# A two-layer hybrid decoder trunk: zero-padded keys, weights in shared half slots, longer hidden groups

## The chip, the cores and the metric

The kernel runs on one core of one Trainium2 chip. The metric is the device time of one execution in microseconds (us), as the median of several runs. A core has five engines that each take instructions in their own order: TensorE (PE, matrix products; its weight loads are shown as PEld), VectorE (DVE), ScalarE (ACT), GpSimdE (POOL) and SyncE (SP, which here issues nearly all DMA transfers). They wait for each other by semaphores.

## What is computed

Two layers (`DEPTH = 2`) on an input of 512 tokens by 1024 features; `c` is a conditioning vector.

```python
for l in range(DEPTH):
    mod = jax.nn.silu(c) @ w_mod[l] + b_mod[l]
    sh1, sc1, g1, sh2, sc2, g2, sh3, sc3, g3 = jnp.split(mod[:, None, :], N_MOD, axis=-1)
    h = _rmsnorm(x) * (1.0 + sc1) + sh1
    x = x + HALF_STEP * g1 * _swiglu(h, ffn1_w_gate[l], ffn1_w_up[l], ffn1_w_down[l])
    h = _rmsnorm(x) * (1.0 + sc2) + sh2
    x = x + g2 * _hybrid_mixer(h, w_in[l], w_out[l], q_norm_g[l], k_norm_g[l], hgrn_norm_g[l], lower_bounds[l])
    h = _rmsnorm(x) * (1.0 + sc3) + sh3
    x = x + HALF_STEP * g3 * _swiglu(h, ffn2_w_gate[l], ffn2_w_up[l], ffn2_w_down[l])
```

`_swiglu` is `(silu(h @ w_gate) * (h @ w_up)) @ w_down` with 2816 hidden features, which are 22 blocks of 128. The mixer projects `h` to 3584 columns and runs three groups of heads: four heads of stick-breaking attention (a, 64 wide), four of dilated attention with normalised and rotated queries and keys (b, 64 wide), four of a gated linear recurrence (c, 128 wide). Their outputs meet in `w_out`.

## The kernel before

**Layout.** Activations lie transposed: features on the 128 partitions, 512 tokens along the free axis. `X` holds the residual stream as eight tiles of 128x512. Every matrix product is made of three (`triple`, line 865): each operand is split into a rounded high part and the remainder, and PE adds high x high, high x low and low x high in one PSUM bank. So a weight that arrives by DMA (tile `w`) needs an ACT copy that makes its high part and a DVE subtraction that makes its low part (tiles `wt`) before PE can use it.

**The program in stages.** `opening` (line 424) reads `x`, transposes it, forms the first layer's shift and scale in four rounds (`row_sums` on PE, `row_products` on DVE, `shift_scale`), modulates (`modulate`), and multiplies the first two pairs of weights (gate and up for blocks 0 and 1). Then come, per layer, a feed-forward network (`ffn`, line 1102), the mixer and a second feed-forward network; the four networks are numbered 0 to 3 in the text.

**A network** works through its 22 hidden blocks in pairs, and the pairs in groups of `GROUP = 6` blocks: 6, 6, 6, 4. For a pair, gate and up products are formed either in the plain way (`dense`: 96 products of 128x512 for gate and up together) or, for the pairs in `FAST`, by `seven` (line 874), which replaces eight block products by seven (168 products of 128x256) at the price of sums of weights and of activations that DVE makes (`combine`, line 943, and the "f" branch of `feed`), and `empty`, which takes the seven results apart. After a group, `down` (line 1212) multiplies its hidden blocks with `w_down` for each of the eight output tiles, and `residual` adds the gated result into `X` on DVE. In the last group the main stream first waits for all hidden blocks, loads the table of ACT functions, and starts the next norm (`start_norm`); its last four output tiles are done in two halves of 256 tokens, so that the norm of the first half can begin early.

**The mixer** starts its first two projections in halves (`first`), then runs the other twelve as filler beside four lanes of head tasks. For a pair of heads, queries and keys lie as one pair of tiles: head 0 in partitions 0 to 63, head 1 in 64 to 127. `stick` and `dilated` take the half that belongs to their head, so that these score products contract over 64 partitions.

**Modulation.** The other shift, scale and gate vectors come from 64 items of 1 MB of `w_mod`. `plan` (line 687) mixes these "mod" items into the list of weights (tables `TAKE` for networks, `TAKE_MIX` for mixers); `background` (line 730) multiplies and adds them on DVE into `acc`, two instructions of 128x1024 per item. A mod item keeps its raw buffer until DVE has done so; while a norm is under way (`hold`), its steps are put back by a bias of 5.0.

**Memory and order.** 37 slots of 4 KB per partition (`SLOTS`) hold activations and split weights (at most `HELD = 11` of them for weights), and three raw buffers of 8 KB (`RAW`) take the loads. `Flow` plays the program through with estimated costs as it is built: of all streams it takes the step that could begin first, with ranks and biases (`BU`, `BF`, `BH`, `BN`) between them. The order of instructions on each engine, the loads on SP too, is what comes out of that. All instructions are recorded by one helper, so that their line in the profile is the same (L111; in the changed kernel L114), and they are told apart by their tiles: `m` and `a` are PSUM banks, `h` the modulated input, `hs` its sums, `u` working tiles, `x` the residual stream.

## Time and profile before

| | |
|---|---|
| runs | 2170.59, 2169.46, 2168.57 us: median 2169.46 us |
| profiled execution | 2170.17 us; first to last instruction (span) 2168.4 us |
| TensorE clock granted, mean | 0.978 |
| PE busy | 2097.1 us (97%), 12592 matmul records |
| DVE busy | 1557.2 us (72%) |
| ACT busy | 979.0 us (45%) |
| POOL busy | 208.4 us (10%) |
| read from HBM | 255.25 MB, 119 GB/s over the span |

Times in the views are microseconds from the span's first instruction. A row of the timeline gives start, length, engine, operation with output and inputs, the count of instructions merged into it, and in brackets how long the engine had been idle before and what released it. A PE row's length includes the run-out of its last product, so paces are best taken from one start to the next. SPq is SP's time in issuing DMAs, waits included.

### The profile page before, as it was taken

What the parts mean: (1) busy time and instruction counts of PE and PEld (TensorE: products, weight loads), DVE (VectorE), ACT (ScalarE), POOL (GpSimd) and SP (SyncE); (2) the same over time, 40 slices, a digit from 0 to 9 for tenths busy, and PEclk for the clock granted to TensorE, in tenths of its full rate; (3) what the DMA queues carried; (4) which work ended last, traced back from release to release, by engine and by line L of the source; (5) the groups of instructions that cost most, each with busy time, mean ns of one, the idle gap of its engine ahead of it and who ended that gap; (6) DMA issues with size and microseconds to landing.
All of it is one profiled execution on the core that took longest, in us unless ns stands there. A gap on an engine that the chain in (4) does not pass through costs nothing.

```text
span 2168.4 us, 30995 instructions
## 1 busy us (share of the span) xinstructions
PE 2097.1 (97%) x12592; PEld 1858.2 (86%) x12592; DVE 1557.2 (72%) x2458; ACT 979.0 (45%) x1642; POOL 208.4 (10%) x235
## 2 busy tenths in 40 slices
PE   7999999899999999999999999998999999999998
PEld 6889989878787888898988989897888779898987
DVE  5866867787688776676785767578878968474665
ACT  3534434545565443433462424355465645242432
POOL 4000000131141100000010000012323201000000
PEclk7999999999999999999999999999999999999999
DMA  9435343353221343434334344333433212332322
GB/s 295 141 128 164 117 155 98 117 207 105 78 93 64 98 135 118 156 104 149 119 115 134 120 136 142 103 126 123 150 117 131 64 59 74 102 103 92 98 88 69
DMA packets 207007, 259.34 MB, mean 120 GB/s; under 512 B 5345, under 2 KB 188533, under 8 KB 206865
## 3 DMA queue, kind: packets, MB, share of 16 engines
q1 hardware_dynamic: 206608, 257.29, 36.4%
q8 instruction: 99, 1.62, 0.3%
q14 instruction: 44, 0.35, 0.0%
q0 software_dynamic: 256, 0.08, 0.0%
HBM read 255.25 MB, written 2.10 MB: 119 GB/s over the span
## 4 chain that ended last, share of the span: by engine, by line
PE 89%; DVE 7%; ACT 2%; DMA 1%; issue 1%; SPq 0%; POOL 0%; DVEq 0%; ACTq 0%
PE m L111 54%; PE a L111 35%; DVE u L111 3%; DVE wt L111 1%; ACT u L111 1%; DVE acc L111 1%; DMA w<-in_w_in_dram 1%; DVE h L111 1%; DVE x L111 0%; DMA u<-in_x_dram 0%; ACT wt L111 0%; DMA w<-in_ffn_w_down_dram 0%; SPq L111 0%; ACT L1351 0%; ACT L111 0%
## 5 line engine op out<-in xcount | busy, mean ns | idle before, releaser
L111 PE MATMUL m<-h,wt 128*128 128x512 f32 (+1 forms) x2928 | 585.5, 352 | 25.9 <-ACT wt L111 9.1
L111 PE MATMUL m<-u,wt 128*128 128x512 f32 (+1 forms) x2640 | 577.5, 376 | 10.7 <-DVE u L111 4.7
L111 PEld LDWEIGHTS m<-u,wt 128*128 128x128 f32 x2640 | 466.9, 190 | 101.8 <-ACT u L111 7.2
L111 PEld LDWEIGHTS m<-h,wt 128*128 128x128 f32 x2928 | 471.8, 195 | 94.6 <-ACT wt L111 9.5
L111 DVE TENSOR_TENSOR wt<-w,wt 128x1024 fp32r<-128x1024 f32 x458 | 502.6, 1112 | 68.2 <-ACT wt L111 67.3
L111 ACT CAST wt<-w 128x1024 fp32r<-128x1024 f32 x460 | 423.9, 950 | 249.2 <-DVE w L111 154.1
L111 PE MATMUL a<-h,wt 128*128 128x256 f32 (+1 forms) x2160 | 366.5, 325 | 0.0
L111 PEld LDWEIGHTS a<-h,wt 128*128 128x128 f32 x2160 | 321.8, 191 | 32.2
L111 DVE TENSOR_TENSOR u<-u 128x256 f32<-128x256 f32 (+4 forms) x448 | 254.9, 589 | 41.0 <-ACT u L111 25.0
L111 POOL TENSOR_TENSOR u<-u 128x256 f32<-128x256 f32 x162 | 140.8, 891 | 1350.5 <-ACT u L111 1104.9
L111 DVE SCALAR_TENSOR_TENSOR x<-m,mod,x 128x512 f32<-128x512 f32 (+1 forms) x168 | 115.1, 686 | 195.0 <-PE m L111 194.7
L111 PE MATMUL a<-hs,wt 128*128 128x256 f32 x1728 | 223.3, 283 | 0.0
L111 PEld LDWEIGHTS a<-hs,wt 128*128 128x128 f32 x1728 | 214.4, 192 | 0.0
L111 PE MATMUL a<-u 128*128 128x64 f32 (+8 forms) x1056 | 162.4, 299 | 5.1 <-DVE u L111 4.4
L111 PEld LDWEIGHTS a<-u 128*128 128x128 f32 (+1 forms) x1056 | 142.9, 193 | 26.9 <-issue 9.3
L111 ACT ACTIVATE u<-u 128x512 f32<-128x512 f32 (+2 forms) x266 | 145.1, 567 | 36.8 <-POOL u L111 14.0
L111 DVE SCALAR_TENSOR_TENSOR acc<-w,sc_c,acc 128x1024 f32<-128x1024 f32 x112 | 145.6, 1300 | 4.6 <-DMA w<-in_w_mod_dram 2.3
L111 ACT COPY u<-m 128x256 f32<-128x256 f32 (+1 forms) x109 | 45.1, 415 | 227.2 <-PE m L111 218.9
L111 ACT CAST u<-u 128x512 fp32r<-128x512 f32 (+1 forms) x105 | 64.5, 617 | 157.6 <-DVE u L111 157.4
L111 DVE TENSOR_TENSOR w<-w 128x512 f32<-128x512 f32 x192 | 131.9, 687 | 3.0
L111 DVE TENSOR_TENSOR u<-u,a 128x256 f32<-128x256 f32 (+1 forms) x88 | 47.3, 539 | 97.7 <-PE a L111 89.6
L111 PE MATMUL m<-wt,h 128*128 128x256 f32 x768 | 100.8, 288 | 5.9 <-DVE u L111 4.8
(136 smaller groups left out, 1382.3 us busy)
## 6 DMA issues: line engine op xcount, KB each, us to landing
w<-in_w_mod_dram SPq DMA_DIRECT2D x64, 1024.0 KB, 5.0
w<-in_ffn_w_gate_dram SPq DMA_DIRECT2D x44, 1024.0 KB, 5.4
w<-in_ffn_w_up_dram SPq DMA_DIRECT2D x44, 1024.0 KB, 5.4
w<-in_ffn_w_down_dram SPq DMA_DIRECT2D x48, 768.0 KB, 4.4
w<-in_w_in_dram SPq DMA_DIRECT2D x28, 1024.0 KB, 5.1
u<-in_w_mod_dram SPq DMA_DIRECT2D x32, 256.0 KB, 6.2
w<-in_ffn_w_down_dram SPq DMA_DIRECT2D x16, 512.0 KB, 3.5
w<-in_w_out_dram SPq DMA_DIRECT2D x8, 512.0 KB, 3.9
```

Of the source, the lines that this page charges most:

```text
L111: ins = fn(*args, **kw)
```

## The change

Five things change, and with them the whole order that `Flow` makes:

1. **Keys per head.** Keys of groups a and b now get one tile per head, with zeros in the rows of the other head (`halves_of_keys`; POOL writes the zeros, ACT and DVE write the 64 rows). The score products contract over all 128 partitions, against the unsplit query tiles.
2. **Raw weights in half slots.** The three raw buffers are gone; a load takes one or two slots of 4 KB from the common pool, now of 43 slots, with at most 8 raw slots in networks and 4 in mixers (`RAW = (8, 4)`). A load of 1 MB becomes two DMAs of 512 KB, each slot is given back by itself, and the split of a "seven" weight follows these halves.
3. **Opening without GpSimd products.** `x * rsqrt` and the second weight's low parts, which POOL made, go to DVE; `modulate` is DVE, ACT, DVE; the splits stand one by one between the rounds.
4. **Modulation with networks only.** 24, 16, 20 and 4 mod items go with networks 0 to 3, spread by a formula, none with the mixers.
5. **Groups 8, 8, 6.** `FAST` has five pairs in network 0 and six in the others, from pair 4 on, and never the last pair. The first two output tiles of each group take the group's last two hidden blocks only after all others (`down_two`), and the table load before a norm is a stream of its own, which the main stream does not wait for. `Flow` also counts PE as slower after a pause.

```diff
-SLOTS = 37
+SLOTS = 43
 RESERVE = 4
-RAW = 3
+RAW = (8, 4)
 HELD = (11, 11)
...
-GROUP = 6
-FAST = ((6, 8, 12, 14, 18, 20),) * 4
+GROUPS = (8, 8, 6)
+FAST = ((4, 8, 12, 16, 18), (4, 8, 10, 12, 16, 18), (4, 8, 10, 12, 16, 18), (4, 8, 10, 12, 16, 18))
...
+MOD_NET = (24, 16, 20, 4)
+EARLY = ((2, 4, 5, 6), (1, 3, 4, 6), (1, 3, 4, 6), (1, 3, 4, 6))
+MOD_MIX = ((0,) * 14,) * 2
...
-            t += self.cost(eng, op, out, ins)
+            if eng == "PE" and t - self.clk[eng] > 1.3:
+                self.cold = t + 3.2
+            t += self.cost(eng, op, out, ins) * (1.9 if eng == "PE" and t < self.cold and out.free_size() > 128 else 1.0)
...
-        xr = [U.get() for _ in range(ND)]
-        for d in range(ND):
-            G.tensor_mul(xr[d], X[d], junk)
...
-            A.activation(t, xr[d], AF.Identity, scale=mod(0, 1, d), bias=mod(0, 0, d))
-            A.copy(hi, t)
-            V.tensor_sub(lo, t, hi)
-            U.put(xr[d])
+            V.scalar_tensor_tensor(t, X[d], mod(0, 1, d), junk, ALU.mult, ALU.mult)
+            A.activation(hi, t, AF.Identity, bias=mod(0, 0, d))
+            V.scalar_tensor_tensor(lo, t, mod(0, 0, d), hi, ALU.add, ALU.subtract)
...
+        split(0, 0)
         modulate(0)
-        split(raw[0], V)
         modulate(1)
-        split(raw[1], G)
...
     def load(i):
-        r = RW.get()
         it = items[i]
...
+        r = [RW.get() for _ in range(slots_of(it))]
+        if it[0] == "mod":
             _, l, j, q = it
...
+            for k in range(2):
+                Q.dma_start(r[k], w_mod[l, (2 * q + k) * P:(2 * q + k + 1) * P, j * D:(j + 1) * D])
+            return r
...
             def down(w, d, cs):
...
+            def down_two(w, cuts):
+
+                yield Step("PE", need=((M, 2),))
+                banks = [M.get() for _ in range(2)]
+                for ks in cuts:
+                    for d, ps in enumerate(banks):
+                        for k in ks:
+                            yield when(keys[k])
+                            hi, lo = hid[k]
+                            wh, wl = part(w, k, d)
+                            yield Step("PE", lo, wh, wl)
+                            triple(ps, wh, wl, hi, lo, k == 0, k == n - 1)
+                        if ks[-1] == n - 1:
+                            F.spawn(residual(key, d, ps, l, jg, FULL), 0)
...
-                for i in range(2):
-                    yield from down(w, d + i, FULL)
+                if d == 0:
+                    yield from down_two(w, (range(n - 2), range(n - 2, n)))
+                else:
+                    for i in range(2):
+                        yield from down(w, d + i, FULL)
...
+        def halves_of_keys(name, hp, src, first):
+
+            tiles = [U.whole(name="k") for _ in range(2)]
+            for j, t in enumerate(tiles):
+                G.memset(t[64 - 64 * j:128 - 64 * j].bitcast(F32), 0.0)
+            for j, t in enumerate(tiles):
+                o = slice(64 * j, 64 * j + 64)
+                first(t[o, :S], src[o])
+            for j, t in enumerate(tiles):
+                o = slice(64 * j, 64 * j + 64)
+                yield Step("DVE", src, t)
+                V.tensor_sub(t[o, S:], src[o], t[o, :S])
+            got[name, hp] = tiles
...
-            qh, ql = (z[r:r + 64] for z in got["qa", hp])
-            kh, kl = (z[r:r + 64] for z in got["ka", hp])
+            qh, ql = got["qa", hp]
+            kt = got["ka", hp][h % 2]
+            kh, kl = kt[:, :S], kt[:, S:]
```

Three places show what becomes of the order; the rows name operation, output and inputs, shape and count.

The first is SP's queue of loads where network 0 ends and the first mixer begins (`w` is a raw buffer, behind the arrow stands the tensor in HBM). Before:

```order
L111 DMA w<-in_w_mod_dram 128x2x1024
L111 DMA w<-in_ffn_w_down_dram 128x4x256 x4
L111 DMA w<-in_w_in_dram 128x8x256
L111 DMA w<-in_w_mod_dram 128x2x1024
L111 DMA w<-in_w_in_dram 128x8x256
L111 DMA w<-in_w_mod_dram 128x2x1024 x2
L111 DMA w<-in_w_in_dram 128x8x256
```

And in the changed kernel:

```order
L114 DMA w<-in_w_mod_dram 128x1024 x2
L114 DMA w<-in_ffn_w_down_dram 128x4x256
L114 DMA w<-in_ffn_w_down_dram 128x2x256
L114 DMA w<-in_ffn_w_down_dram 128x4x256
L114 DMA w<-in_ffn_w_down_dram 128x2x256
L114 DMA w<-in_ffn_w_down_dram 128x4x256
L114 DMA w<-in_ffn_w_down_dram 128x2x256
L114 DMA w<-in_w_in_dram 128x4x256 x28
```

The mod loads that stood between the projections' weights are gone: all 28 halves of the fourteen projections follow each other.

The second is DVE in the opening, from the first shift and scale (`mod`) to the third; `acc` is a row product, `h` the low part of the modulated input, `wt` the low part of a weight. Before:

```order
L111 TENSOR_TENSOR mod_94<-a,bcol_96 128x2x2
L111 TENSOR_TENSOR h<-u,h 128x512
L111 TENSOR_TENSOR wt<-w,wt 128x1024 x2
L111 TENSOR_TENSOR h<-u,h 128x512
L111 TENSOR_SCALAR acc<-u,sc_c 128x512
L111 SCALAR_TENSOR_TENSOR acc<-u,sc_c,acc 128x512 x4
L111 TENSOR_TENSOR mod_94<-a,bcol_96 128x2x2
L111 TENSOR_TENSOR h<-u,h 128x512 x2
L111 TENSOR_SCALAR acc<-u,sc_c 128x512
L111 SCALAR_TENSOR_TENSOR acc<-u,sc_c,acc 128x512 x5
L111 TENSOR_TENSOR mod_94<-a,bcol_96 128x2x2
```

And in the changed kernel, up to the second:

```order
L114 TENSOR_TENSOR mod_91<-a,bcol_93 128x2x2
L114 TENSOR_TENSOR wt<-w,wt 128x1024
L114 SCALAR_TENSOR_TENSOR u<-x_83,mod_91,u 128x512
L114 SCALAR_TENSOR_TENSOR h<-u,mod_91,h 128x512
L114 SCALAR_TENSOR_TENSOR u<-x_84,mod_91,u 128x512
L114 SCALAR_TENSOR_TENSOR h<-u,mod_91,h 128x512
L114 TENSOR_TENSOR wt<-w,wt 128x1024
L114 TENSOR_SCALAR acc<-u,sc_c 128x512
L114 SCALAR_TENSOR_TENSOR acc<-u,sc_c,acc 128x512 x4
L114 TENSOR_TENSOR mod_91<-a,bcol_93 128x2x2
```

Each modulated tile now takes two instructions of DVE, where it took one.

The third is PE at the end of network 0: the first two output tiles of the last group (banks `m_3324` and `m_3344` before, `m_3273` and `m_3274` after; behind the arrow a hidden block `u`, then the high and the low part of a half of `w_down`, `wt`). Before, each bank takes the group's four blocks in a row:

```order
L111 MATMUL m_3324<-u_3127,wt_3182 128x512 x2
L111 MATMUL m_3324<-u_3127,wt_3183 128x512
L111 MATMUL m_3324<-u_3150,wt_3182 128x512 x2
L111 MATMUL m_3324<-u_3150,wt_3183 128x512
L111 MATMUL m_3324<-u_3317,wt_3182 128x512 x2
L111 MATMUL m_3324<-u_3317,wt_3183 128x512
L111 MATMUL m_3324<-u_3303,wt_3182 128x512 x2
L111 MATMUL m_3324<-u_3303,wt_3183 128x512
L111 MATMUL m_3344<-u_3127,wt_3182 128x512 x2
```

And in the changed kernel, from the fourth of the group's six blocks in the second bank:

```order
L114 MATMUL m_3274<-u_3097,wt_3116 128x512 x2
L114 MATMUL m_3274<-u_3097,wt_3117 128x512
L114 MATMUL m_3273<-u_3231,wt_3181 128x512 x2
L114 MATMUL m_3273<-u_3231,wt_3182 128x512
L114 MATMUL m_3273<-u_3281,wt_3181 128x512 x2
L114 MATMUL m_3273<-u_3281,wt_3182 128x512
L114 MATMUL m_3274<-u_3231,wt_3181 128x512 x2
L114 MATMUL m_3274<-u_3231,wt_3182 128x512
L114 MATMUL m_3274<-u_3281,wt_3181 128x512 x2
L114 MATMUL m_3274<-u_3281,wt_3182 128x512
```

The last pair's two blocks (`u_3231`, `u_3281`) now stand behind 24 products of the other four; before, the last pair's two (`u_3317`, `u_3303`) stood behind six.

## The prediction, made before the change was run

> **What bounds the kernel now.** I read the page's totals and chain first, then stretches of the span by windows, then the PE rows of the timeline where those stretches fall short.

> ```profile
> PE 2097.1 (97%) x12592; PEld 1858.2 (86%) x12592; DVE 1557.2 (72%) x2458; ACT 979.0 (45%) x1642; POOL 208.4 (10%) x235
> PE 89%; DVE 7%; ACT 2%; DMA 1%; issue 1%; SPq 0%; POOL 0%; DVEq 0%; ACTq 0%
> ```

> PE carries 89% of the chain. But a busy PE need not be at its pace, so I took the pace from two links of the chain, and then one network against the two mixers (columns: length, then busy time of PE, PEld, DVE, ACT, POOL, then the granted clock):

> ```profile
> 92.80 10.88 PE m L111 x48
> 157.54 10.08 PE a L111 x84
> 120.00:378.00 258.00, 258.00 (x1615) 234.42 (x1614) 183.74 (x287) 105.10 (x168) 0.00 (x0) 1.00 0.41 132
> 440.00:730.00 290.00, 281.53 (x1629) 239.76 (x1628) 234.81 (x415) 156.54 (x280) 67.34 (x81) 0.95 0.34 113
> 1500.00:1790.00 290.00, 279.57 (x1647) 238.15 (x1648) 236.51 (x422) 157.78 (x287) 68.85 (x76) 0.97 0.33 109
> ```

> 48 products of 512 columns in 10.88 us are 0.2267 us each; 84 of 256 columns in 10.08 are 0.120. The difference gives 0.417 us per 1000 columns and 13 ns per product; "at pace" means this below. Network 0 is full, at clock 1.00: there only fewer columns help. The mixers lack 8.5 and 10.4 us of PE and run at clock 0.95 and 0.97: 290 x 0.05 + 290 x 0.03 is another 23 us. So what can be won lies in the mixers, at their starts, at the networks' ends and in the opening.

> **The change part by part.** The sum is made against the profiled execution, 2170.2 us, which is 0.7 above the median.

> *Keys per head.* PE gets as many products and columns, over 128 rows in place of 64.

> ```profile
> L111 PE MATMUL a<-u 64*128 64x512 f32 x48 | 12.8, 460 | 0.0
> 548.12 0.80 PE L111 MATMUL a<-u 64*128 64x384 f32 x3
> 551.70 1.75 PE L111 MATMUL a<-u 128*128 128x512 f32 x5
> 695.63 0.55 PE L111 MATMUL a<-u 64*128 64x128 f32 x3
> 696.11 0.96 PE L111 MATMUL m<-u,wt 128*128 128x512 f32 x3
> 671.74 2.17 PE L111 MATMUL a<-u 64*128 64x512 f32 x15
> 673.84 1.66 PE L111 MATMUL m<-u,wt 128*128 128x512 f32 x6
> ```

> A stick head's scores (from 548.12 to 551.70: four triples of 64 rows and four 128-column products between them) take 3.58 us. At pace they are 3 x 1280 columns x 0.417/1000 + 12 x 0.013 + 4 x 0.112 = 2.3, so 1.24 are lost; eight heads make 9.9. A lone dilated triple (695.63 to 696.11) takes 0.48 against 3 x 0.067 = 0.20; with the entry I call it 0.35 (an estimate), and some ten per mixer make 3.5. The burst of fifteen goes the other way: 2.10 us against 15 x 0.2267 = 3.40, so its loss of 1.3 per mixer is the change's. Together -9.9 - 7.0 + 2.6 = **-14** (bounds: all of the first two, -17; the sticks' without their strict products, -8).

> [...]

> *The clock behind those bursts.*

> ```profile
> 500.00:530.00 30.00, 29.94 (x190) 25.58 (x188) 25.30 (x40) 17.11 (x32) 1.57 (x1) 0.92 0.46 147
> 530.00:560.00 30.00, 30.00 (x133) 24.32 (x132) 16.58 (x32) 20.31 (x38) 5.32 (x8) 0.86 0.07 29
> 560.00:600.00 40.00, 37.51 (x186) 31.57 (x186) 29.15 (x44) 20.45 (x34) 10.31 (x13) 0.91 0.32 106
> 1590.00:1620.00 30.00, 30.00 (x136) 24.63 (x136) 21.82 (x36) 22.07 (x38) 7.28 (x9) 0.89 0.37 127
> ```

> Where the stick heads run, the granted clock falls to 0.86 to 0.92, in 530 to 560 with PE busy throughout. Time lost: 30 x 0.08 + 30 x 0.14 + 40 x 0.09 + 30 x 0.11 = 13.5. If 64-row products count as little work to what grants the clock, full-height ones end this; the window of 560 also has 2.5 us of idle PE. I take half, **-7** (0 to -13.5).

> [...]

> *Mixer starts.* This is where SP's queue changes.

> ```profile
> 389.12 14.52 SPq L111 DMA_DIRECT2D w<-in_w_mod_dram  x2
> 420.04 0.37 SPq L111 DMA_DIRECT2D w<-in_w_in_dram  x1
> 424.88 5.92 PE L111 MATMUL a<-h,wt 128*128 128x256 f32 x48
> 435.35 1.22 PE L111 MATMUL m<-h,wt 128*128 128x512 f32 x2 [4.54 <-ACT wt L111]
> 438.89 12.64 PE L111 MATMUL m<-h,wt 128*128 128x512 f32 x46 [2.33 <-DVE wt L111]
> 451.38 0.30 PE L111 MATMUL a<-p,quads 128*128 128x32 f32 x2
> 1487.13 5.92 PE L111 MATMUL a<-h,wt 128*128 128x256 f32 x48
> 1501.08 10.98 PE L111 MATMUL m<-h,wt 128*128 128x512 f32 x40 [2.37 <-DVE wt L111]
> 1511.90 0.30 PE L111 MATMUL a<-p,quads 128*128 128x32 f32 x2
> ```

> Two mod loads hold raw buffers through the norm, the third projection's weight is only asked for at 420.04, and PE stands for 4.54 and 2.33 us, then runs slow. From the end of `first` (430.80) to 451.38, 48 products take 20.58 us; at pace 10.88, so 9.7 are lost. In the second mixer 1493.05 to 1511.90 holds 42: 18.85 - 9.52 = 9.3. With no mod items there, this weight's halves are the next two in SP's queue, and their split stands ahead of the gate chain. I take all, **-19**; if the split is late by one of the two waits it is -8. Late next would be the fourth projection's weight, which has 10.88 us of PE to hide in.

> *Mixers without mod items.* 32 items leave, of two DVE instructions each:

> ```profile
> L111 DVE SCALAR_TENSOR_TENSOR acc<-w,sc_c,acc 128x1024 f32<-128x1024 f32 x112 | 145.6, 1300 | 4.6 <-DMA w<-in_w_mod_dram 2.3
> L111 DVE SCALAR_TENSOR_TENSOR x<-m,mod,x 128x512 f32<-128x512 f32 x128 | 95.9, 750 | 177.1 <-PE m L111 176.8
> w<-in_ffn_w_down_dram SPq DMA_DIRECT2D x16, 512.0 KB, 3.5
> ```

> 16 x 2 x 1.30 = 42 us of a mixer's 235 of DVE. What the mixers lack in PE (8.5 + 10.4) is mostly PE waiting on head tasks. I take about half, **-9** (0 to -19; above nothing, +5, if the new order puts some head task later).

> *The same items in networks.* Network 0 goes from 12 to 24: 31 us more on DVE, (184 + 31)/258 = 83%; PE covers it. Without that cover they cost their own length, which is the first rival. Half-slot loads double the DMAs, 512 KB each, which land in 3.5 us; SP has few other things to do. I set **+2** for late halves (0 to +10).

> *Network ends.*

> ```profile
> 377.31 1.55 PE L111 MATMUL m<-u,wt 128*128 128x512 f32 x6
> 380.33 0.49 PE L111 MATMUL m<-u,wt 128*128 128x512 f32 x1 [1.47 <-ACT u L111]
> 381.42 12.63 PE L111 MATMUL m<-u,wt 128*128 128x512 f32 x53 [0.59 <-DVE u L111]
> 2135.87 2.17 PE L111 MATMUL m<-u,wt 128*128 128x512 f32 x7
> 2138.26 2.81 PE L111 MATMUL m<-u,wt 128*128 128x512 f32 x11 [0.23 <-DVE u L111]
> ```

> Network 0: 377.31 to 381.42 is 4.11 for 7 products, 1.59 at pace: 2.5 lost. In the last network 2.39 against 1.59: 0.8. Taking networks 1 and 2 for like network 0: 8.3, and about 1 of slow products after. Now 24 products of the other blocks stand first, 5.4 us against the 4.1 that the last pair needed: **-9** (-11 to -3, if one bank's change costs a wait of its own).

> *One fast pair fewer, more halves.* A dense pair's 96 x 0.2267 = 21.8 replaces 168 x 0.120 = 20.2: +1.6. At the networks' ends two more blocks go through the halved output tiles: 72 products of 512 become 144 of 256, 17.3 - 16.3 = +1.0. **+2.6**. Network 0's first fast pair comes one pair sooner, while DVE also makes the eight low parts of `hs` (687 ns each):

> ```profile
> L111 DVE TENSOR_TENSOR hs<-u,hs 128x512 fp32r<-128x512 f32 x32 | 22.0, 687 | 6.2 <-ACT hs L111 6.2
> ```

> PE could wait for all (5.5) or none of them; **+1.5**.

> *Opening.*

> ```profile
> 16.39 4.88 DVE L111 SCALAR_TENSOR_TENSOR acc<-u,sc_c,acc 128x512 f32<-128x512 f32 x4
> 34.21 5.07 DVE L111 SCALAR_TENSOR_TENSOR acc<-u,sc_c,acc 128x512 f32<-128x512 f32 x4
> 45.48 3.90 DVE L111 SCALAR_TENSOR_TENSOR acc<-u,sc_c,acc 128x512 f32<-128x512 f32 x5
> 17.35 12.63 POOL L111 TENSOR_TENSOR u<-x,u 128x512 f32<-128x512 f32 x8 [11.81 <-ACT u L111]
> ```

> While POOL multiplies, four row products take 4.88 and 5.07; undisturbed five take 3.90, so four 3.12. That gives back 3.7. Other DVE work beside POOL may gain as much again, so 7 in all is the bound. Against it stand eight more DVE instructions in `modulate`, by the nearest row 0.75 each, 6.0, most of which the chain of rounds passes, and two low parts of weights. ACT's copy leaves the chain. I take **-3** (-7 to +6).

> Sum: -14 - 7 - 19 - 9 + 2 - 9 + 2.6 + 1.5 - 3 = -55, so 2115 us; against the median's scale 2114.

> **The rivals.**

> (1) *Slower: the weights of fast pairs come late.* 23 fast pairs take two weights each, split half by half from a common pool in which 8 raw slots, 11 held ones and the activations leave none to spare, and DVE's queue holds 12 more mod items in network 0. If a half's slot comes free only when PE already wants the product, each of 46 weights is late by a landing, 3.5 us: +161 - 55, 2276 us. From 55/46 = 1.2 us per weight the change is slower. For it speaks DVE's 83%; against it, that PE's 258 us in network 0 show no gap with DVE at 71%.

> (2) *The mixers are bound by head tasks.* Then PE's gains inside them (14 + 7 + 9) only lengthen waits, and -25 is left: 2145. For it: PE lacks 8.5 and 10.4 us there, with DVE busy 81%. Against it: the relief of 42 us of DVE.

> (3) *All clock loss and most waits of the mixers go.* The clock term -13.5 and the relief -19 make 16.5 more: 2098. For it: the idle of 560 to 600 lies behind the same heads. Against it: clock 0.89 stands in one window of the second mixer only.

> (4) *The mixer starts do not change*, because the split, not the load, is late: -8 for -19, 2126; within the forecast's own range.

> (5) *The clock falls after pauses only*, and 64-row products have no part in it: the clock term is 0, 2122, also within that range. For it: the idle of 560 to 600. Against it: the full window of 530 at 0.86.

> **How the numbers follow.** The forecast proper has 0.35, (3) 0.20, (2) 0.19, (4) and (5) 0.10 each, (1) 0.06. Less than 0.2% (4.3 us) can't be told from no change. Faster 0.94: all but (1) and a little of (2); same 0.02; slower 0.04, as a part of (1) stays below 1.2 us. The forecast's own terms spread by some 14 us to either side (the bounds of the six largest, taken as independent); the range reaches to (2) above, and below past (3), where the opening and the relief may give their bounds too: 2086 to 2146.

> **What would show it.** Steps right: no 64-row rows; sticks' scores in 2.3 us; clock at least 0.95 in the sticks' windows; no wait over 1 us on `wt` at the mixers' starts; no wait on `u` after six products at networks' ends; networks at clock 1.00 without gaps; DVE near 195 us in a mixer's stretch; the first pair of network 0 some 3 us sooner. Wrong: PE idle on DVE `wt` or on a DMA of gate or up weights within networks (rival 1); as many us of PE idle in mixers as were won (rival 2); a clock that stays at 0.86 beside full-height products.

## The result and the profile after

The changed kernel takes 2110.24 us (2109.16 to 2111.56), the kernel before 2170.03 us beside it; the ratio is 0.9721, 95% interval 0.9705 to 0.9738. The forecast was 2114, with 2086 to 2146 as range. The profiled execution took 2111.56 us.

The page of the changed kernel: the engines' busy time, and the chain by engine.

```profile
PE 2062.4 (98%) x12592; PEld 1845.5 (87%) x12592; DVE 1536.6 (73%) x2416; ACT 970.8 (46%) x1613; POOL 191.2 (9%) x236
PE 90%; DVE 7%; ACT 2%; issue 1%; DMA 1%; SPq 0%; ACTq 0%; DVEq 0%
```

PE still carries the chain, with as many products. The mean granted clock was 0.978 over a span of 2168.4 us before; the span and the clock after:

```profile
core 0: 2109.8 us, clock 0.992
```

2168.4 x 0.022 = 47.7 us and 2109.8 x 0.008 = 16.9 us are lost to a slow clock, as far as PE had work then: at most 31 of the 58.6 us that the span lost are clock. By the granted clock in the trace, some 14 us of the loss before lay where the stick heads run, some 9 at the two mixer starts, and some 12 at the ends of networks and mixers and in the norms. At the starts, the ends and in the norms the slow stretches stand behind waits: in the 3.41 us ahead of each of them PE was busy for 0.14 to 1.69 us only. The rest of the gain is PE that no longer stands still.

To place the gain, I took for every product the time from its start to the next one's, less its pace (0.2267 us for 512 columns, 0.120 for 256, and so on), and added this excess by stretch (us). Where one stretch ends and the next begins is partly a choice; other borders move up to 3 us from one row to its neighbour.

| stretch | before | after | difference | the prediction's terms |
|---|---|---|---|---|
| opening | 32.7 | 28.1 | -4.7 | -3 |
| ends of networks | 12.2 | 0.1 | -12.1 | -9 |
| norms between stages | 20.0 | 16.6 | -3.4 | 0 |
| starts of the two mixers | 19.3 | 1.5 | -17.8 | -19 |
| the two mixers | 56.8 | 19.3 | -37.5 | -14 - 7 - 9 = -30 |
| inside networks | 0 | 14.2 | +14.2 | +2 + 1.5 = +3.5 |
| more columns | | | +2.6 | +2.6 |
| sum | | | -58.7 | -55 |

Four views of the changed kernel carry this. First the two mixers by windows (columns as in the prediction), the first line of each pair where the stick heads run:

```profile
500.00:560.00 60.00, 59.90 (x350) 53.26 (x349) 43.91 (x78) 44.51 (x81) 8.82 (x12) 1.00 0.17 53
440.00:720.00 280.00, 272.34 (x1735) 242.92 (x1734) 210.22 (x408) 163.88 (x304) 71.41 (x89) 0.99 0.20 65
1530.00:1590.00 60.00, 59.90 (x358) 53.62 (x357) 44.82 (x80) 44.14 (x80) 8.83 (x12) 1.00 0.14 47
1472.00:1752.00 280.00, 271.46 (x1728) 242.59 (x1727) 207.32 (x407) 163.85 (x304) 70.82 (x88) 0.99 0.20 65
```

The sticks run at clock 1.00, where it was 0.86 to 0.92; DVE is busy 210 and 207 us, not 235.

Then PE's timeline at the first mixer's start and at network 0's end:

```profile
422.06 5.92 PE L114 MATMUL a<-h,wt 128*128 128x256 f32 x48
427.82 7.44 PE L114 MATMUL m<-h,wt 128*128 128x512 f32 x32
```

```profile
366.77 11.49 PE L114 MATMUL m<-u,wt 128*128 128x512 f32 x50
```

The third projection follows the second without a pause (422.06 + 48 x 0.120 = 427.82), where PE stood 4.54 and 2.33 us. The products of `down` run on, 50 in 11.3 us plus the run-out.

And what is new, PE's waits inside the networks:

```profile
91.85 1.33 PE L114 MATMUL m<-hs,wt 128*128 128x256 f32 x9 [1.17 <-ACT u L114]
277.51 0.41 PE L114 MATMUL a<-p,quads 128*128 128x32 f32 x2 [1.08 <-DVE p L114]
813.32 0.41 PE L114 MATMUL a<-p,quads 128*128 128x32 f32 x2 [2.83 <-DVE p L114]
1175.71 5.05 PE L114 MATMUL m<-u,wt 128*128 128x512 f32 x21 [1.50 <-DVE x L114]
1846.88 1.44 PE L114 MATMUL m<-u,wt 128*128 128x512 f32 x5 [2.04 <-DVE x L114]
```

The first is the first fast pair. In the others a vector of shift, scale or gate is being finished: PE has the small product of its last step (`quads`) in its queue before DVE's sum `p` is there, or waits for a bank whose `residual` waits for the gate vector. Before, half of the mod items went with the mixers, and no such wait stood in a network.

### The profile page after: what moved, and what is told of

Its sections match the earlier page's. It is cut to its first block, busy times and chain, and to the rows that moved or that the text cites. A ratio compares the mean times of both kernels' runs of the same rounds, so it can differ in the third digit from the quotient of the medians.

```text
span 2109.8 us, 31726 instructions
## 1 busy us (share of the span) xinstructions
PE 2062.4 (98%) x12592; PEld 1845.5 (87%) x12592; DVE 1536.6 (73%) x2416; ACT 970.8 (46%) x1613; POOL 191.2 (9%) x236
## 4 chain that ended last, share of the span: by engine, by line
PE 90%; DVE 7%; ACT 2%; issue 1%; DMA 1%; SPq 0%; ACTq 0%; DVEq 0%
PE m L114 55%; PE a L114 35%; DVE u L114 2%; DVE wt L114 1%; ACT u L114 1%; DVE acc L114 1%; DVE h L114 1%; ACT wt L114 1%; DVE x L114 1%; DMA w<-in_ffn_w_down_dram 0%; ACT h L114 0%; DVE k L114 0%; DVE c L114 0%; DMA u<-in_x_dram 0%; DVE p L114 0%
## 5 line engine op out<-in xcount | busy, mean ns | idle before, releaser
L114 PE MATMUL m<-h,wt 128*128 128x512 f32 (+1 forms) x2940 | 581.3, 348 | 11.1 <-DVE h L114 5.5
L114 DVE TENSOR_TENSOR wt<-w,wt 128x1024 fp32r<-128x1024 f32 (+1 forms) x440 | 504.9, 1154 | 114.4 <-ACT wt L114 103.6
L114 ACT CAST wt<-w 128x1024 fp32r<-128x1024 f32 (+1 forms) x440 | 423.8, 979 | 340.1 <-PE m L114 149.2
L114 PE MATMUL a<-h,wt 128*128 128x256 f32 (+1 forms) x2172 | 373.2, 327 | 0.0
L114 PE MATMUL a<-hs,wt 128*128 128x256 f32 x1656 | 213.7, 283 | 0.0
L114 PEld LDWEIGHTS a<-hs,wt 128*128 128x128 f32 x1656 | 205.3, 192 | 0.0
L114 DVE SCALAR_TENSOR_TENSOR x<-m,mod,x 128x512 f32<-128x512 f32 (+1 forms) x136 | 90.8, 670 | 121.6 <-PE m L114 121.4
L114 PEld LDWEIGHTS a<-u 128*128 128x128 f32 x864 | 115.2, 191 | 15.1 <-DVE u L114 3.3
L114 ACT CAST u<-u 128x512 fp32r<-128x512 f32 x98 | 60.7, 620 | 133.2 <-DVE u L114 125.3
L114 PE MATMUL a<-u 128*128 128x64 f32 (+4 forms) x864 | 117.3, 282 | 4.0 <-DVE u L114 2.9
L114 ACT COPY u<-a 128x256 f32<-128x256 f32 (+2 forms) x132 | 52.1, 394 | 112.7 <-PE a L114 111.8
## 6 DMA issues: line engine op xcount, KB each, us to landing
w<-in_w_mod_dram SPq DMA_DIRECT2D x128, 512.0 KB, 4.4
w<-in_ffn_w_gate_dram SPq DMA_DIRECT2D x88, 512.0 KB, 4.8
w<-in_ffn_w_up_dram SPq DMA_DIRECT2D x88, 512.0 KB, 4.8
w<-in_ffn_w_down_dram SPq DMA_DIRECT2D x80, 512.0 KB, 4.6
w<-in_w_in_dram SPq DMA_DIRECT2D x56, 512.0 KB, 4.5
```

What stands on the lines that cost most here:

```text
L114: ins = fn(*args, **kw)
```

## The experiments

All start from the changed kernel (2110.24 us). Medians are of four runs; the kernel before took 2169.7 to 2171.0 beside them.

**Score products over 64 rows again** (2134.95 us, ratio 0.9841 [0.9817, 0.9866]).

```diff
-            qh, ql = got["qa", hp]
-            kh, kl = kt[:, :S], kt[:, S:]
+            r = 64 * (h % 2)
+            qh, ql = (z[r:r + 64] for z in got["qa", hp])
+            kh, kl = kt[r:r + 64, :S], kt[r:r + 64, S:]
```

(The same for group b.)

> The changed kernel with one thing put back: the score products of groups a and b contract over the 64 rows of their head again. The key tiles with their zeros, all of DVE's and POOL's work and the order on every engine stay as they are, so only the form of 192 products differs. Theory of the prediction: entering and leaving 64-row products costs 14 us, and the clock that falls around the stick heads 7 more: 2131 us (2124 to 2138), with the granted clock at 0.86 to 0.92 where the stick heads run. Rival (5), the clock falls after pauses only: 2124, clock 1.00 there. Rival (2), the mixers are bound by the head tasks: at most 2115, PE's extra time taken from its idle time. Rival (3): the clock is worth all 13.5: 2138.

24.7 us more, with the same instructions in the same order on every engine. The start of the first two stick heads of this run and what follows them on PE (rows between are left out), and then the same in the changed kernel:

```profile
504.62 0.78 PE L114 MATMUL a<-u,k 64*128 64x384 f32 x3
505.59 0.55 PE L114 MATMUL a<-u,k 64*128 64x128 f32 x3
514.55 5.35 PE L114 MATMUL m<-h,wt 128*128 128x512 f32 x15
519.74 0.33 PE L114 MATMUL a<-u,nones_r 128*128 128x128 f32 x2
```

```profile
506.90 0.68 PE L114 MATMUL a<-u,k 128*128 128x384 f32 x3
507.48 0.50 PE L114 MATMUL a<-u,k 128*128 128x128 f32 x3
511.55 3.63 PE L114 MATMUL m<-h,wt 128*128 128x512 f32 x15
515.02 0.34 PE L114 MATMUL a<-u,nones_r 128*128 128x128 f32 x2
```

504.62 to 514.55 is 9.93 us; full-height it is 4.65. And the fifteen ordinary products behind them take 5.19 us in place of 3.47: they are the same products, on a slower clock. The windows of this run:

```profile
500.00:530.00 30.00, 30.00 (x135) 23.49 (x133) 16.07 (x30) 17.64 (x33) 1.77 (x3) 0.83 0.00 1
530.00:560.00 30.00, 30.00 (x142) 24.50 (x142) 18.78 (x36) 22.58 (x41) 4.87 (x8) 0.89 0.13 38
504.49:507.90 3.41, 3.41 (x16) 2.32 (x15) 0.01 (x1) 1.41 (x3) 0.00 (x0) 1.00 0.00 0
507.90:518.14 10.24, 10.24 (x27) 7.31 (x27) 5.34 (x10) 6.26 (x13) 0.62 (x1) 0.50 0.00 0
1550.00:1580.00 30.00, 30.00 (x135) 23.09 (x133) 15.84 (x33) 19.37 (x39) 2.29 (x3) 0.89 0.00 1
```

The profile shows PE busy throughout all five, and the clock is half of full speed for 10.24 us. The loss in the three windows of 30 us is 30 x 0.17 + 30 x 0.11 + 30 x 0.11 = 11.7 us. Of the 25.0 us that the mixers' products take longer in this run's trace, product by product, some 13 are left for the 64-row products and the ones next to them: the first triple and the 128-column product behind it take 0.97 us at clock 1.00 (504.62 to 505.59), full-height 0.58 (506.90 to 507.48). So both parts of the theory stand, rival (5) falls (the clock falls here without a pause in the profile, and not when the same products are full-height), and rival (2) too: PE's time in the mixers came back almost whole.

**Mod items back in the mixers, from the fifth projection on** (2132.88 us, 0.9836 [0.9816, 0.9857]), **and with the list of before** (2146.57 us, 0.9901 [0.9872, 0.9930]).

```diff
-MOD_NET = (24, 16, 20, 4)
-MOD_MIX = ((0,) * 14,) * 2
+MOD_NET = (12, 10, 10, 0)
+MOD_MIX = ((0, 0, 0, 0, 2, 2, 2, 2, 2, 2, 1, 1, 1, 1),) * 2
```

```diff
-MOD_NET = (24, 16, 20, 4)
-MOD_MIX = ((0,) * 14,) * 2
+MOD_NET = (12, 10, 10, 0)
+MOD_MIX = ((1, 2, 1, 2, 1, 1, 1, 1, 1, 1, 1, 1, 1, 1),) * 2
```

> The changed kernel with 16 mod items back in each mixer, from the fifth projection on, none with the first four; networks 0 to 3 keep 12, 10, 10 and 0. Theory of the prediction: 42 us of DVE come back into each mixer and cost 9 us over both, while PE's waits in the networks for finished vectors (about 7 us in the changed kernel: 1.1, 2.8, 1.5, 2.0 us idle) mostly go: 2108 to 2115. Rival: DVE's relief had no part in the mixers' gain, which came from the full-height products and the order: about 2103. Rival: the head tasks wait for DVE behind every item: 2125 and more.

> As the run with the 16 items late in the mixers, but with the list of before: 1, 2, 1 and 2 items behind the first four projections, one behind each of the others. Theory of the prediction: those first items keep raw slots through the norm, the third projection's weight comes late again, and PE loses 9.7 and 9.3 us at the mixers' starts: 19 above the run with late items, some 2130. Rival: the halves that are given back singly, and the split ahead of the gate chain, keep the starts free whatever the list: as the run with late items, within 4 us.

The first expectation was far off: 22.6 us more, the last of its three cases. With two items behind a projection, DVE's queue holds what a head task needs behind them. PE in this run, and DVE just before the end of that wait:

```profile
648.25 2.07 PE L114 MATMUL m<-wt,h 128*128 128x256 f32 x8 [6.62 <-DVE u L114]
```

```profile
637.63 3.18 DVE L114 SCALAR_TENSOR_TENSOR acc<-w,sc_c,acc 128x1024 f32<-128x1024 f32 x2
642.06 1.22 DVE L114 TENSOR_TENSOR wt<-w,wt 128x1024 fp32r<-128x1024 f32 x1
647.78 0.75 DVE L114 TENSOR_TENSOR u<-m,u 128x256 fp32r<-128x256 f32 x2
```

From 637.63 to 648 DVE has no pause and PE has nothing else. The two items take 3.18 us of that, splits of weights and steps of head tasks the rest. The run with the list of before takes 13.7 us more than this one (19 were expected), and both starts are back as they were. PE, and then SP's queue, with that list:

```profile
430.59 1.22 PE L114 MATMUL m<-h,wt 128*128 128x512 f32 x2 [4.54 <-ACT wt L114]
434.21 11.96 PE L114 MATMUL m<-h,wt 128*128 128x512 f32 x42 [2.39 <-DVE wt L114]
```

```profile
398.54 0.82 SPq L114 DMA_DIRECT2D w<-in_w_mod_dram  x2
412.65 4.30 SPq L114 DMA_DIRECT2D w<-in_w_mod_dram  x4
417.32 0.93 SPq L114 DMA_DIRECT2D w<-in_w_in_dram  x2
```

The waits are those of before to the last digit or two (4.54 and 2.33), the third projection's weight is again asked for behind mod loads, and the excess at the two starts is 10.1 and 9.4 us. So it was the list, not the half slots, that freed the starts. The rest of the two mixers has 34.8 us of excess here against 20.8 (19.3 and the starts' 1.5): the same list as before costs 14.0 us inside the mixers, in waits, most of them on DVE, and in slow products behind them. With both lists the networks were to get their waits back. With the list of before little came of that: at network 1's first fast pair (786 us) the weights are late, and 7.4 us of excess are new there.

**Without the two cuts; the last pair fast; both** (2105.73 us, 0.9709 [0.9688, 0.9731]; 2110.35 us, 0.9729 [0.9712, 0.9746]; 2108.45 us, 0.9717 [0.9699, 0.9735]).

```diff
-                if d == 0:
-                    yield from down_two(w, (range(n - 2), range(n - 2, n)))
+                if False:
+                    pass
```

```diff
-FAST = ((4, 8, 12, 16, 18), (4, 8, 10, 12, 16, 18), (4, 8, 10, 12, 16, 18), (4, 8, 10, 12, 16, 18))
+FAST = ((4, 8, 12, 16, 20), (4, 8, 10, 12, 16, 20), (4, 8, 10, 12, 16, 20), (4, 8, 10, 12, 16, 20))
```

> The changed kernel without the first two output tiles' two cuts: each bank takes all blocks of its group in a row again. The groups 8, 8, 6 and the dense last pair stay. Theory of the prediction: the last pair's blocks are wanted after 12 products, 2.7 us, and were ready after 4.1: about 1.4 us lost at each of four network ends, and the slow products behind it: 2114 to 2118, with a wait on u after 12 products. Rival: a dense last pair is ready in time, so that its being dense and not the two cuts removed the stalls: 2110, no wait. Upper end, if the groups inside a network stall too: 2122.

> The changed kernel with the last fast pair of each network moved from 18 to 20, so that the last pair is fast, as before the change; the first two output tiles keep their two cuts. Theory A, the two cuts can hide a fast pair's end: 24 products, 5.4 us, stand before the last pair's blocks, which were ready 4.1 us on: no wait on u at the networks' ends, 2106 to 2112. Theory B, the dense last pair alone removed those stalls: waits of some 2 us come back at four ends, 2116 to 2120.

> As the run with the last pair fast, and each bank takes its group's blocks in a row again, without the two cuts. With the run without cuts and a dense last pair (2105.7, no wait) this makes the four cases of cut and last pair. Theory: either of the two hides the end, and only without both do the stalls come back: 12 products, 2.7 us, against 4.1, so 1.4 us and slow products behind, 6 to 10 us over four ends: 2112 to 2118 with a wait on u. Rival C: the table load that no longer holds the main stream, or the longer group, removed the stalls: no wait on u here either, 2105 to 2108.

The cuts alone buy nothing: without them, and with the dense last pair, no product of `down` waits for `u` at a network's end. (The 4.5 us that the run is faster by are no more than its interval; in its trace the wait for `p` at 813 has gone, since the order shifted.) A fast last pair does not matter with the cuts. Without both, small waits come, as expected though smaller than 1.4 us; PE at network 0's end in that third run:

```profile
365.38 3.14 PE L114 MATMUL m<-u,wt 128*128 128x512 f32 x13
368.95 3.24 PE L114 MATMUL m<-u,wt 128*128 128x512 f32 x13 [0.44 <-DVE u L114]
```

0.7 to 1.1 us at each of four ends, 3.5 together. So each of the two hides what little is left, and neither is where 12.1 us came from.

**Groups 6, 6, 6, 4, with the fast pairs of before and without cuts** (2121.48 us, 0.9782 [0.9764, 0.9801]).

```diff
-GROUPS = (8, 8, 6)
-FAST = ((4, 8, 12, 16, 18), (4, 8, 10, 12, 16, 18), (4, 8, 10, 12, 16, 18), (4, 8, 10, 12, 16, 18))
+GROUPS = (6, 6, 6, 4)
+FAST = ((6, 8, 12, 14, 18, 20),) * 4
```

(Without the cuts, as above.)

> The changed kernel with the groups 6, 6, 6, 4, the fast pairs of before (the last one too) and no cuts: at a network's end everything is as before the change but the table load, which is a stream of its own and doesn't hold the main stream. Theory: the length of the last group decides; with four blocks only 6 products, 1.4 us, stand before the last pair's, so 2.5 us are lost again at three or four ends and up to 1 us of slow products behind: against the run with six blocks (fast, without cuts, 0.6 to 0.8 lost per end) +7, and -2.6 for one more fast pair and fewer halves: 2111 to 2114. Rival: the main stream's wait for all hidden blocks and the table load made the stalls: then 0.7 per end here too, 2103 to 2107.

PE at network 0's end:

```profile
381.99 1.55 PE L114 MATMUL m<-u,wt 128*128 128x512 f32 x6
386.14 0.50 PE L114 MATMUL m<-u,wt 128*128 128x512 f32 x1 [2.61 <-ACT u L114]
386.87 3.51 PE L114 MATMUL m<-u,wt 128*128 128x512 f32 x14 [0.22 <-DVE u L114]
```

The stall is back at all four ends, 15.7 us of excess, though the table load is a stream of its own; so that load was not the cause. The length of the last group is one cause: six products (1.4 us) stand before the last pair's blocks with four blocks, twelve (2.7 us) with six. It is not the only one. PE can go on with the last pair's blocks 4.88 us after the start of `down` here (381.99 to 386.87), 3.57 us after it in the third run above (365.38 to 368.95), and 4.11 before the change. Here and before the change the last two pairs, 18 and 20, are both fast; in that third run pair 18 is dense. So some 1.3 us of this stall come from blocks that are ready later, and whether the neighbouring fast pairs make them so was not tried alone. The total is above the expectation by 7 us, about the 7.6 us of excess that this order has in the middle of network 0, which the expectation left out: there the weights behind a fast pair are late.

```profile
281.80 0.73 PE L114 MATMUL m<-h,wt 128*128 128x512 f32 x2 [2.44 <-ACT wt L114]
```

**The opening with POOL's products** (2110.72 us, 0.9741 [0.9715, 0.9766]).

```diff
+        xr = [U.get() for _ in range(ND)]
+        for d in range(ND):
+            G.tensor_mul(xr[d], X[d], junk)
...
-            V.scalar_tensor_tensor(t, X[d], mod(0, 1, d), junk, ALU.mult, ALU.mult)
-            A.activation(hi, t, AF.Identity, bias=mod(0, 0, d))
-            V.scalar_tensor_tensor(lo, t, mod(0, 0, d), hi, ALU.add, ALU.subtract)
+            A.activation(t, xr[d], AF.Identity, scale=mod(0, 1, d), bias=mod(0, 0, d))
+            A.copy(hi, t)
+            V.tensor_sub(lo, t, hi)
+            U.put(xr[d])
...
-            V.tensor_sub(lo, rv, hi)
+            (G if which else V).tensor_sub(lo, rv, hi)
```

The sums of activations that network 0's fast pairs use then hold the shift twice; their instructions and time are the same.

> The changed kernel with the opening's arithmetic put back: POOL multiplies x by rsqrt in eight products and makes the second weight's low parts, and a modulated tile takes two of ACT and one of DVE; the splits' places stay. Theory of the prediction: POOL's products slow the row products on DVE from 3.1 to some 4.9 us for four, twice, and the opening ends 3 us later (at most 7): 2113, products ending some 3 us later than the changed kernel's. Rival: fewer DVE instructions on the chain of rounds outweigh that: 2104 to 2108. In both, a row of four row products beside POOL's takes over 4.5 us, and one without under 3.5.

In this run, DVE's first and third row products and POOL's work beside them; then DVE's first in the changed kernel:

```profile
15.38 4.88 DVE L114 SCALAR_TENSOR_TENSOR acc<-u,sc_c,acc 128x512 f32<-128x512 f32 x4
39.23 7.96 DVE L114 SCALAR_TENSOR_TENSOR acc<-u,sc_c,acc 128x512 f32<-128x512 f32 x5
16.34 14.07 POOL L114 TENSOR_TENSOR u<-x,u 128x512 f32<-128x512 f32 x8 [10.79 <-ACT u L114]
39.10 5.18 POOL L114 TENSOR_TENSOR wt<-w,wt 128x1024 fp32r<-128x1024 f32 x2 [8.69 <-ACT wt L114]
```

```profile
15.88 3.12 DVE L114 SCALAR_TENSOR_TENSOR acc<-u,sc_c,acc 128x512 f32<-128x512 f32 x4
```

Four take 4.88 beside POOL and 3.12 without, five 7.96 and (in the prediction's rows) 3.90. So DVE's row products take longer while POOL works. Yet the end tells little of it. The first product after the opening's stands at 67.94 us here, at 65.58 in the changed kernel and at 70.40 before:

```profile
67.94 0.23 PE L114 MATMUL a<-ident,tpar 14*128 14x14 f32 x1
```

```profile
65.58 0.23 PE L114 MATMUL a<-ident,tpar 14*128 14x14 f32 x1
```

So POOL's arithmetic is worth about half of the opening's 4.8 us; the other half may lie in where the splits stand, which was not tried alone. In the total even the 2.4 us do not show (2110.72 for 2110.24): the first fast pair, which waits at 91.85 in the changed kernel, waits 0.9 us less when the opening ends later, and behind the wait at 813 the clock does not fall (in the changed kernel it is 0.50 from 814.47 to 817.89 us), which is 1.3 us less.

**Six raw slots in networks** (2122.75 us, 0.9788 [0.9770, 0.9807]).

```diff
-RAW = (8, 4)
+RAW = (6, 4)
```

> The changed kernel with at most 6 raw slots in networks in place of 8, which is the memory of the three raw buffers of before, still loaded and given back by halves. Rival (1) of the prediction lives on late raw slots: if they are near the limit, loads start later and PE waits for gate and up weights: 10 us and more, 2120 to 2150. Theory: the halves' early return gives room, loads stay ahead of PE by more than their landing: 2106 to 2114.

12.5 us more. PE in network 1, at its first fast pair:

```profile
768.02 0.50 PE L114 MATMUL a<-h,wt 128*128 128x256 f32 x2 [1.34 <-ACT wt L114]
771.27 0.50 PE L114 MATMUL a<-hs,wt 128*128 128x256 f32 x2 [1.08 <-ACT wt L114]
773.92 4.40 PE L114 MATMUL a<-hs,wt 128*128 128x256 f32 x22 [2.14 <-DVE wt L114]
```

The same stands in networks 2 and 3, 7.3 to 8.3 us of excess each, 22.9 together. The total is up by less because the waits for finished vectors (277, 813, 1175 and 1846 in the changed kernel, some 10 us) are gone in this order. Rival (1) had the right mechanism: with the memory of the three old raw buffers, the new list and the new groups make the weights of a fast pair late. Two more slots of 4 KB keep it out.

**Towards a faster version.** Without the cuts in each; then the gate vectors' items sooner in networks 2 and 3 (2113.07 us, 0.9739 [0.9721, 0.9757]), or the last network's items with network 2 (2101.80 us, 0.9691 [0.9672, 0.9710]), or network 0's first fast pair later (2104.80 us, 0.9703 [0.9681, 0.9726]).

```diff
-EARLY = ((2, 4, 5, 6), (1, 3, 4, 6), (1, 3, 4, 6), (1, 3, 4, 6))
+EARLY = ((2, 4, 5, 6), (1, 3, 4, 6), (1, 3, 4, 5), (0, 1, 2, 3))
```

```diff
-MOD_NET = (24, 16, 20, 4)
+MOD_NET = (24, 16, 24, 0)
```

```diff
-FAST = ((4, 8, 12, 16, 18),
+FAST = ((6, 8, 12, 16, 18),
```

> A version that may beat both: the changed kernel without the two cuts, and with the mod items of the gate vector earlier in the third and the fourth network (behind the weights 1, 3, 4, 5 and 0, 1, 2, 3, for 1, 3, 4, 6). In the run without cuts PE lost 4.0 us in the fourth network (1845 us) and 0.5 in the third (1174), waiting for a residual that waits for its gate vector. Theory: the vector is done before the first group's end, and those 4 us go: 2100 to 2103. Rival: the earlier items take raw slots from the first weights, and PE waits there as much: 2105 to 2108.

> A version that may beat both: without the two cuts, and the last four mod items (the last network's gate vector) go with the third network (24, 16, 24, 0). Theory: the residual at the fourth network's first group no longer waits for its gate vector (4.0 us in the run without cuts) and nothing takes its place, as DVE has room in the third network: some 2102. Rival: the third network's DVE queue gets late and gives back as much: 2106 and more.

> Without the two cuts, and the first network's fast pairs at 6, 8, 12, 16, 18: its first fast pair one pair later, where it was before the change. Theory of the prediction's term (+1.5 for the sooner pair; 1.4 us of excess at 90 us in the changed kernel): that wait goes, 2104. Rival: pairs 6 and 8 then stand next to each other while the mod items are densest, and DVE is late for the second: 2107 and more.

The first is slower than either of its expectations. The wait for the gate vector in the fourth network has gone, but the first fast pair there asks for its up weight only at 1780.61 us, where the run without cuts asks at 1771.95. Its rival's reading, that sooner items hold the raw slots, fits; the cost is 11.1 us of excess at that one place:

```profile
1788.62 2.50 PE L114 MATMUL m<-h,wt 128*128 128x256 f32 x10 [2.24 <-DVE wt L114]
```

With no items in the last network the waits for its gate vector go and nothing takes their place. The windows of that run, and of the changed kernel, where the last network's first `down` begins (at 1825.8 and 1833.6 us):

```profile
1825.00:1850.00 25.00, 25.00 (x112) 20.70 (x111) 11.73 (x14) 5.64 (x7) 0.00 (x0) 1.00 0.36 121
```

```profile
1825.00:1850.00 25.00, 22.95 (x103) 18.71 (x102) 17.74 (x21) 6.29 (x7) 0.00 (x0) 1.00 0.64 201
```

Its 2101.8 us (2100.2 to 2102.5) are the fastest of all and beat both kernels; it has 10.3 us less excess in its trace than the changed kernel. The later fast pair's 1.4 us go too, but its total can't be told from the run without cuts.

## Why the prediction was right, and where its steps were off

**What bounds the kernel.** Right: network 0 was full before, and there nothing was gained. Nearly all gains lie in the stretches named; 3.4 us came in the norms, which it did not name.

**Keys per head, -14, and the clock behind the bursts, -7.** Right in mechanism. Measured by undoing them: some 13 and 11.7. The clock term was halved for the idle PE in the window of 560, and should not have been: 13.5 us were counted, and 11.7 came with the 64-row products alone. Three figures behind the -14 were off, and nearly cancel. The terms given for a stick head's scores add up to 2.2 us, not 2.3; the 2.3 that was used is what a head measures (4.65 / 2). The burst of fifteen is twelve products of 512 columns and three of 384, 3.24 us at pace, not 3.40. And a lone triple of 64 rows costs 0.2 to 0.3 us more than a full-height one, product by product in the two traces, not 0.35.

**Mixer starts, -19.** Right: -17.8, and 19.6 of excess came back with the old list. Rival (4) falls.

**Mixers without mod items, -9.** Too small: 14.0 by the run with the old list, within the bounds. "About half" of PE's missing time was a guess, and more of it went. DVE's time in the first mixer's stretch fell from 235 to 210 us (in windows of 290 and 280 us), not by 42: the stretch of 440 to 730 held only 26 of the 32 instructions, 33.6 us, and other work fills some of the room.

**Network ends, -9.** The size was nearly right (-12.1), the reason wrong. The step said that 24 products of the other blocks now stand first. The cuts that put 24 there are worth nothing; a last group of six blocks already puts twelve ahead, and a dense last pair does the rest. With four blocks and two fast pairs at the end the whole loss returns, and more; 1.4 us of each stall is the shorter group.

**The items in networks, +2, and the first fast pair, +1.5.** The step that failed. The second is 1.4 us, as said. But the first was sized as late half loads, with DVE's length as the only other price. No wait over 1 us in its networks is for a gate or up weight. What came is PE waiting for a vector's last small product, or for the residual behind it, and slow products after: 10.5 us in four places, and 2.3 in short waits of half a microsecond. A term for moved work has to follow the moved chain to its consumer: here DVE's sum, two products on PE, four more on DVE, then the residual that gives a bank back.

**Opening, -3.** -4.7, half of it POOL's arithmetic.

The norms between stages, for which no term stood, gave 3.4; some 2 to 3 of it went again when the mod items were back in the mixers with the list of before. The terms' errors, -7.5 in the mixers, -3 each at norms and ends, -2 in the opening, +1 at the starts and +11 in networks, cancel to -4. That the 2110 is nearer to the forecast than its steps are is luck.

**The rivals.** (1) is real but lies two raw slots away. (2) fell with the first experiment. (3) came true for the clock and for two thirds of the waits; its 2098 lacks the networks' new waits.

## What to carry to other kernels

Where TensorE is the bound, sum each product's start-to-start time less its pace by stretch, and read the granted clock beside it: here up to half of the gain was clock (at most 31 of 58.6 us), and some 14 us of that lay around the stick heads, where windows showed PE busy with hardly a gap (30.00 of 30.00 us from 530 at clock 0.86). Background work that leaves a stage takes its last step with it, so look at who consumes the result, not only at the busy share of the engine that receives it. And when several edits aim at one stall, undo them one at a time: the one written for the network ends did nothing that a longer last group with a dense last pair had not done.

## What the hardware showed unexpectedly

The traces can tell these two apart. In every trace the stretches at half clock last 3.41 us or a multiple of it (6.83, 10.24, 13.65; the last one is cut off by the end), so I cut all fourteen traces, behind the opening, into such steps. For each step at full clock I summed the work of the products that start in it, at pace (0.111 us for products of up to 128 columns), and looked at the clock of the next step. (In the openings of the two kernels half clock also followed full-height steps of 2.1 to 2.9 us of work, with many products of one column in them.) Behind the opening, with full-height products alone, all 40 steps with less than 1.3 us of work were followed by half clock, and none of the 238 with 1.55 to 2.55 us was. With 64-row products among them, 7 of the 12 steps with 1.55 to 2.55 us were. So the height counts: for the clock, a 64-row product was worth less than a full-height one of as many columns. Two rows of the 64-row run's windows, 504.49 and 507.90, show one such step and the half clock behind it: 15 products start in it, 2.2 us of work. In the changed kernel 13 full-height products start in a step, 1.8 us of work with PE idle for 1.02 us, and the next step stays at full clock:

```profile
1664.40:1667.81 3.41, 2.39 (x15) 1.76 (x14) 3.40 (x6) 3.01 (x5) 2.36 (x3) 1.00 0.46 154
1667.81:1671.22 3.41, 3.41 (x31) 3.41 (x30) 3.29 (x6) 1.97 (x4) 1.11 (x2) 1.00 0.25 82
```

A gain from the short contractions was there too. Twelve 64-row products of alternating heads (six of 512 columns and six of 384) took 1.42 us in the run with 64 rows, and 2.46 over 128 rows in the changed kernel:

```profile
1696.70 1.50 PE L114 MATMUL a<-k,u 64*128 64x512 f32 x12
1698.12 0.96 PE L114 MATMUL m<-u,wt 128*128 128x512 f32 x3
```

```profile
1675.83 2.62 PE L114 MATMUL a<-k,u 128*128 128x512 f32 x12
1678.29 0.86 PE L114 MATMUL m<-u,wt 128*128 128x512 f32 x3
```

So here 64 rows paid in a long burst of both halves (1.42 us for 2.46) and cost in lone triples (0.2 to 0.3 us each); this kernel had more of the latter.
